# Small partition moves as maxima, weight halves by stage, and new prices in the ordering clock of a two-layer encoder

## The chip, the cores and the metric

The kernel runs on one core of a Trainium2 chip. The metric is the device time of one execution in microseconds (us), given as the median of several runs. A profiled execution of the same kernel gives the trace. The core's engines are named as in the profile: PE (matrix multiply, with PEld for its weight loads), DVE (VectorE), ACT (ScalarE), POOL (GpSimd) and SP (which issues the DMAs). Each engine works through its own instructions in order, and engines wait for each other by semaphores.

## The reference

Two layers of an encoder over 512 tokens of width 1024, in float32. Each layer, cut to what matters here:

```python
h = rms_norm(x, attn_norm_g)
c_q, c_kv, k_rope, gq, gk, gv, pool_in, gate_logits = split_columns(h @ w_in, IN_SIZES)
o_mla  = mla_branch(...)     # 8 heads, q and k of 96, v of 64, from latents of 256 and 128
o_gqa  = gqa_branch(...)     # 8 query heads, 2 key heads of 64
o_pool = pool_branch(...)    # centred means over 2, 4, 8, 16 tokens, minus the token
gates  = sigmoid(gate_logits)
merged = gates[0]*(o_mla @ w_b0) + gates[1]*(o_gqa @ w_b1) + gates[2]*(o_pool @ w_b2)
x = x + merged @ w_out
u_gate, u_val = split(depthwise_conv(rms_norm(x, ffn_norm_g) @ w_up))   # width 3, 2 x 2816 channels
x = x + (silu(u_gate) * u_val) @ w_down
```

Each attention computes `softmax(q k^T * scale) v` per head over all 512 keys.

## The kernel before

**Arithmetic.** Every float32 operand of a product is split into a high part, rounded by a copy to the format that PE reads in one pass, and a low part, the difference. A product is then three matmuls (`mm3`: high by high, high by low, low by high). Weights arrive from HBM in tiles `raw` and are split on the chip in `w_split`: `wh` by an ACT copy, `wl` by a subtraction on POOL or DVE. `pick` chooses the engine of `wl` from the modelled times at which the two come free, with `W_BIAS` in POOL's favour. `wnext` hands out one weight tile and keeps three more prepared ahead (`LA`).

**Stages of a layer.** In order: the latent projection, four pooling channels, the projections of the grouped-query attention (GQA), then the GQA heads, then the eight heads of the latent attention (MLA), then the output projection, then the feed-forward part. Beside the heads of both attentions runs a *filler*: units of three matmuls each that compute branch gates (`gate`) and branch projections (`branch`). A filler unit is put in wherever the heads have nothing ready. Some 48 further units follow the MLA heads.

**The order is made beforehand.** The instruction order of each engine is written out while the kernel is built. An ordering clock (`Clock`, and `Engine`, which wraps DVE, ACT and POOL) keeps a modelled time for PE and for each engine. `took` adds an instruction's modelled cost to its engine, `done` notes when a result will be there, and `chain` queues the steps of a chain of small instructions behind each other. `copy` puts a copy on ACT or DVE, whichever would end first by the model, with `C_BIAS` in ACT's favour. None of this is an instruction; it only decides which instruction comes after which, and on which engine. A matmul is priced at its columns divided by 2370, in us, and not below 0.107.

**An MLA head** is issued by `held_banks`, a list of tasks with conditions. Each round issues the first task that may go by the model; if none may, one filler unit is put in; if the filler has none left, modelled time passes with nothing issued. For head `h`:

- `a_part(h, k)`, four of them (line 1307): the high-by-high score product of one block of 128 keys into a PSUM bank, which stays held. Afterwards DVE takes maxima of it (`largest`, a transposing reduction, tile `nmt`).
- Behind the fourth: `over_keys` (maximum over the blocks, line 250), `gather` (three copies of 32 partitions by 16 values from the other three partition groups to the group in which the row is wanted, line 258), `over_groups` (a further maximum, tile `mrow`) and `row` (a DVE product that spreads the negated maxima into `qb`, line 242).
- `b_part(h, k)` (line 1348): two further products per bank; they need `qb` because the maximum is subtracted inside the product. They may be issued 0.4 us of modelled time after `qb` is due.
- `weights`: exponential on ACT, high copy `ph`, low part `pl`, and `vt` on DVE, which then releases the bank.
- `av_hi`, `av_lo`, `av_rest`: products with the values, 0.4 to 1.2 us after their operands are due.

`a_part` of the next head follows `b_part` of this one, and may not go before a quota of filler units is used. The quota is spread over the heads so that `late` units, the second number of `LEAD`, are left when the last head begins. Other work of a head on POOL: `qb` (low part of the queries), `kl` (low part of the keys) and `oraw` (a sum in the head's output). Lines 235, 242, 246, 250, 258, 266 are the helpers that record every ACT, DVE and POOL instruction; line 389 records nearly all matmuls.

Of the kernel before, what the change touches and what calls it, by code (L numbers as in the profile page):

```python
# [14 lines left out]
ALU = mybir.AluOpType  # L15
AX = mybir.AxisListType
PSUM = bass.MemoryType.PSUM

P = 128
T = 512  # L20
D = 1024
KC = D // P
# [22 lines left out]
RSQRT_BITS = 1597463007.0  # L45
SLACK = 35
PLAN = {"gqa": (-4.2, -1.0, -0.2, 0.0, 0.65, 2.411, 4.57, 32.003)}
LEAD = {"mla": (1.2, 22)}

D_OUT, D_IN, D_LAT = 3.2, 4.0, 6.0  # L50
D_FREE, D_SUM = 0.8, 2.0
REST = 0.4
W_BIAS = 2.54
C_BIAS = 0.2

PRM_AG, PRM_FG, PRM_PS, PRM_CQ, PRM_CKV = 0, 8, 16, 20, 22
PRM_W0 = 23
# [53 lines left out]
class Filler:  # L111


    def __init__(self, gen, total):
        self.gen, self.total, self.done = gen, total, 0
# [18 lines left out]
class Clock:  # L134
# [5 lines left out]
    def __init__(self):  # L140
        self.now, self.n, self.heap, self.busy = 0.0, 0, [], False
        self.fin, self.free, self.ready = 0.0, {}, {}
        self.source = self.last = None
        self.gives_way = {}

    def low(self, fn, most=4.0, engine="DVE"):
        self.gives_way[fn] = (engine, most)
        return fn
# [2 lines left out]
        heapq.heappush(self.heap, (self.now + dt, self.n, fn))  # L151
        self.n += 1

    def took(self, engine, cost):
        start = self.now + (0.0 if self.source is None else 0.13 if self.source == engine else self.SEM)
        self.free[engine] = max(start, self.free.get(engine, 0.0)) + cost
        self.last = engine
        self.fin = max(self.fin, self.free[engine])

# [17 lines left out]
    def done(self, *key):  # L177
        self.ready[key] = self.fin + self.SEM
# [36 lines left out]
class Engine:  # L215
# [4 lines left out]
    def __init__(self, ck, eng, kind):  # L220
        self.ck, self.eng, self.kind, self.table = ck, eng, kind, 0

    def _count(self, ap, per, fixed):
        n = 1
        for d in ap.shape[1:]:
            n *= d
        self.ck.took(self.kind, fixed + per * n)

    def activation(self, out, in_, func, **k):
        t = self.TABLE.get(func)  # L230
        if t and t != self.table and not (t == 2 and func is AF.Tanh and self.table == 3):
            self.table = t
            self.ck.took(self.kind, 1.28)
        self._count(out, 0.00084, 0.09 + 0.09 * (len(k) > 0))
        return self.eng.activation(out, in_, func, **k)  # L235

    def _two(self, out, *a):
        self._count(out, *((0.14, 0.1) if ALU.pow in a else (0.002145, 0.127) if self.kind == "Pool" else (0.00105, 0.07)))

    def tensor_tensor(self, out, *a):  # L240
        self._two(out, *a)
        return self.eng.tensor_tensor(out, *a)  # L242

    def scalar_tensor_tensor(self, out, *a):
        self._two(out)
        return self.eng.scalar_tensor_tensor(out, *a)  # L246

    def tensor_reduce(self, out, in_, *a, **k):
        self._two(in_)
        return self.eng.tensor_reduce(out, in_, *a, **k)  # L250

    def tensor_scalar(self, out, *a):
# [1 line left out]
        return self.eng.tensor_scalar(out, *a)  # L254

    def tensor_copy(self, out, in_, psum=False):
        self._count(out, 0.00105 if psum else 0.00053, 0.07)
        return self.eng.tensor_copy(out, in_)  # L258

    def reciprocal(self, out, in_):  # L260
# [13 lines left out]
def trunk(ctx: ExitStack, tc: tile.TileContext, x, w, prm, gb, cst, pad, out):  # L274
    nc = tc.nc
    ctx.enter_context(tc.manual_schedule())
    ck = Clock()
    at, need, done, chain, low = ck.at, ck.need, ck.done, ck.chain, ck.low
    V, A, G = Engine(ck, nc.vector, "DVE"), Engine(ck, nc.scalar, "ACT"), Engine(ck, nc.gpsimd, "Pool")
# [48 lines left out]
    def f(ap):  # L328
        return ap.bitcast(F32)
# [2 lines left out]
    pieces, swidth = _stream()  # L332
    soff = np.concatenate([[0], np.cumsum(swidth)]) * P
    st = {"dma": 0, "split": 0, "use": 0}
    raws, halves = {}, {}

    def w_dma():
        i = st["dma"]
        t = slot("raw") if i < KC else rawp.tile([P, 1024], F32, tag="raw", name=f"raw{i}")
        SY.dma_start(t[:, :swidth[i]], w[int(soff[i]):int(soff[i + 1])].rearrange("(p c) -> p c", p=P))  # L340
        raws[i] = t
        st["dma"] += 1

    def w_split():
        j = st["split"]
        sl, off, wd = pieces[j]
        while st["dma"] <= sl:
            w_dma()
        r = raws[sl][:, off:off + wd]
        hi = hlp.tile([P, T], F32R, tag="wh", name=f"wh{j}")  # L350
        lo = hlp.tile([P, T], F32R, tag="wl", name=f"wl{j}")
        ck.fin = ck.now
        if j == 0:
            V.tensor_copy(hi[:, :wd], r)
        else:
            A.activation(hi[:, :wd], r, AF.Copy)
        e = V if j < KC else G if j < KC + 3 else pick(W_BIAS, ck.fin + ck.SEM)
        ck.free[e.kind] = max(ck.free.get(e.kind, 0.0), ck.fin + ck.SEM)
        e.tensor_tensor(lo[:, :wd], r, f(hi[:, :wd]), ALU.subtract)
        done("w", j)  # L360
        if j + 1 == len(pieces) or pieces[j + 1][0] > sl:

            at(max(0.0, ck.free[e.kind] - ck.now) + D_FREE, lambda: w_upto(sl + 1 + RAW))
        halves[j] = (hi, lo)
        st["split"] += 1

    def pick(bias, t=0.0):

        t = max(t, ck.now)
        dve, pool = (max(t, ck.free.get(e, 0.0)) for e in ("DVE", "Pool"))  # L370
        return V if dve + 0.61 + bias < pool + 1.18 else G
# [15 lines left out]

    def mm(o, lhsT, rhs, start, stop):
        PE.matmul(o, lhsT=lhsT, rhs=rhs, start=start, stop=stop)  # L389
        ck.to(ck.now + max(0.107, rhs.shape[-1] / 2370.0))  # L390

    def turn(o, src):
        PE.transpose(o, src, ident)
        ck.to(ck.now + 0.107)

    def mm3(o, lh, ll, rh, rl, start, stop):
        mm(o, lh, rh, start, False)
# [118 lines left out]

    def copy(out, in_, psum=True, bias=C_BIAS):

# [40 lines left out]
    def layer(l, sq, xsrc):  # L559
# [194 lines left out]
        for b in range(4):  # L754
            v = slot("vg", F32R)
# [144 lines left out]
        now_mla = [False]  # L900
# [266 lines left out]
        def attention(kind, fill, okey, odst):  # L1167
# [135 lines left out]
            def a_part(h, k):  # L1303
                s = hs[h]
                tag, sc = sc_bank()
                s["sc", k] = (tag, sc)
                PE.matmul(sc, lhsT=s["ka"][:, k * P:k * P + P], rhs=s["qa"][:, :T], start=True, stop=True)
                ck.to(ck.now + T / 2370.0)
                if k == 0:
                    both = small("nmt", [P, P], bufs=1)  # L1310
                    s["pm"], s["pk"] = (both[:, c:c + 64].rearrange("p (k j) -> p k j", j=16) for c in (0, 64))
                base = 64 if gqa else 96

                def largest():
                    V.tensor_reduce(s["pm"][:, k], sc.rearrange("p (j r) -> p j r", r=32), AX.X, ALU.max,
                                    apply_transpose=True)

                def over_keys():
                    s["row"] = small("mrow", [P, 16], bufs=1)
                    V.tensor_reduce(s["pk"][:, 3], s["pm"].rearrange("p k j -> p j k"), AX.X, ALU.max)  # L1320

                def gather():
                    for g in range(4):
                        if 32 * g != base:
                            V.tensor_copy(s["pk"][base:base + 32, g if g < 3 else base // 32], s["pk"][32 * g:32 * g + 32, 3])

                def over_groups():
                    V.tensor_reduce(s["row"][base:base + 32], s["pk"][base:base + 32].rearrange("p g j -> p j g"), AX.X, ALU.max,
                                    negate=True)

                def row():
                    V.tensor_tensor(s["qb"][base:base + 32, :T].rearrange("p (j r) -> p j r", r=32),
                                    bc(s["row"][base:base + 32].unsqueeze(2), [32, 16, 32]),
                                    bc(ident[base:base + 32, None, base:base + 32], [32, 16, 32]), ALU.mult)
                    done(*key("m", h))

                chain(largest, *[over_keys, gather, over_groups, ([key("q", h)], row)] * (k == 3), after=0.3)

            def b_part(h, k):
                s = hs[h]  # L1340
                need(key("m", h), key("q", h))
                if not gqa:
                    need(key("kl", h))
                tag, sc = s.pop(("sc", k))
                kb_ = slice(k * P, k * P + P)
                pairs = [("kb", "qb")] if gqa else [("kb", "qa"), ("ka", "qb")]
                for n, (a_, b_) in enumerate(pairs):
                    PE.matmul(sc, lhsT=s[a_][:, kb_], rhs=s[b_][:, :T], start=False, stop=n == len(pairs) - 1,  # L1348
                              skip_group_check=True)
                    ck.to(ck.now + T / 2370.0)  # L1350
                weights(h, k, sc, lambda: sc_free(tag))

            def probs(h, k):
# [73 lines left out]
            def o_out(h):  # L1427
# [25 lines left out]

                steps = [low(copies, 1.5, "ACT") if kind in LEAD else copies]
                if h % 2 == 1:
# [15 lines left out]
            def held_banks():  # L1471
# [4 lines left out]

                lead, late = LEAD[kind]
                step = (fill.total - fill.done - late) / 7.0
# [133 lines left out]
        fb.upto(PRE_B)  # L1612
        while not ck.has(("tq", l, 0)) and fb.step():
            pass
        now_mla[0] = True
        attention("mla", fb, "om", omla)
        rest[0].finish()


        sq = slot("sq")  # L1620
# [56 lines left out]
        n = 0  # L1677
# [250 lines left out]
```

## Time and profile before

| what | value |
|---|---|
| median of 3 runs | 1572.32 us (1570.05 to 1575.77) |
| profiled execution | 1572.05 us |
| its span, first to last instruction | 1570.3 us, mean granted PE clock 0.999 |
| busy, share of the span: PE, DVE, ACT, POOL | 99%, 64%, 50%, 66% |
| HBM read and written | 151.50 MB and 13.63 MB, 105 GB/s |

A profile page gives the busy time of each engine, the groups of instructions by source line, and the waits. Its times are of one execution. A row of a group reads: line, engine, operation, output tile<-input tiles, shapes, count, then busy time and the mean of one in ns, then how long the engine stood idle before them and for whom. A row of a wait reads: engine, its tile and line, whom it waited for, then us in total, how often, and the longest. Durations of neighbouring instructions on one engine can overlap by a few hundredths of a us, and a matmul is drawn longer than its distance to the next.

### The profile page before, as it was taken

How to read it: one execution, taken by the hardware profiler on the slowest of the kernel's cores; microseconds unless marked ns; L12 is line 12 of the kernel's file. 1: busy time of each engine (PE TensorE's matmuls, PEld its weight loads, DVE VectorE, ACT ScalarE, POOL GpSimd, SP SyncE). 2: the span in 40 equal slices, each digit the busy share in tenths (PEclk: the TensorE clock that was granted, in tenths of full speed). 3: DMA queues.
4: the chain of work that ended last, by engine and by line, in shares of the span. 5: the costliest groups of instructions: out<-in, count | busy, mean ns of one | idle time of the engine just before them, and what ended most of it. 6: DMA issues, size and time to landing. Idle time of an engine off the chain costs nothing. (4 is left out here: it accounts for less than half of the span.)

```text
span 1570.3 us, 20451 instructions
## 1 busy us (share of the span) xinstructions
PE 1548.3 (99%) x7034; PEld 1288.0 (82%) x7034; DVE 1008.8 (64%) x1471; ACT 788.6 (50%) x1460; POOL 1032.4 (66%) x918
## 2 busy tenths in 40 slices
PE   9999999899999999999999999999999999999999
PEld 8878787778888888888898888877788888888888
DVE  6778889996267777711046788899862777776000
ACT  6557866664444444432244687756533444444221
POOL 4866986655667666654578669767546766666542
PEclk9999999999999999999999999999999999999999
DMA  5432234324323223333335222433252232332331
GB/s 201 126 113 74 75 111 141 101 91 136 106 94 100 100 97 94 94 120 109 114 106 135 93 79 70 147 116 112 69 157 98 86 102 94 96 100 99 108 129 46
DMA packets 82855, 166.46 MB, mean 106 GB/s; under 512 B 20928, under 2 KB 42944, under 8 KB 82752
## 3 DMA queue, kind: packets, MB, share of 16 engines
q1 hardware_dynamic: 82464, 165.03, 34.1%
q8 instruction: 55, 0.90, 0.2%
q14 instruction: 48, 0.39, 0.1%
q10 hardware_dynamic: 288, 0.14, 0.0%
HBM read 151.50 MB, written 13.63 MB: 105 GB/s over the span
## 5 line engine op out<-in xcount | busy, mean ns | idle before, releaser
L242 POOL TENSOR_TENSOR wl<-raw,wh 128x512 fp32r<-128x512 f32 (+2 forms) x499 | 671.0, 1356 | 356.5 <-ACT wh L235 331.6
L235 ACT ACTIVATE wh<-raw 128x512 fp32r<-128x512 f32 (+2 forms) x521 | 309.1, 607 | 122.7 <-PE ps_ST L389 41.3
L246 DVE SCALAR_TENSOR_TENSOR a<-u,prm,a 128x511 f32<-128x511 f32 x176 | 246.4, 1401 | 93.0 <-ACT a L235 86.1
L389 PE MATMUL ps_acc<-HH,wl 128*128 128x512 f32 x592 | 230.9, 390 | 0.4 <-POOL wl L242 0.4
L389 PE MATMUL ps_acc<-HH,wh 128*128 128x512 f32 x592 | 231.3, 391 | 0.0
L389 PE MATMUL ps_acc<-HL,wh 128*128 128x512 f32 x592 | 230.9, 390 | 0.0
L389 PEld LDWEIGHTS ps_acc<-HH,wl 128*128 128x128 f32 x592 | 111.3, 188 | 24.3 <-POOL wl L242 0.9
L389 PEld LDWEIGHTS ps_acc<-HH,wh 128*128 128x128 f32 x592 | 111.5, 188 | 22.9 <-issue 0.3
L389 PEld LDWEIGHTS ps_acc<-HL,wh 128*128 128x128 f32 x592 | 111.4, 188 | 22.9
L242 POOL TENSOR_TENSOR al<-a,ah 128x512 fp32r<-128x512 f32 x44 | 57.8, 1314 | 84.9 <-ACT ah L235 84.9
L389 PE MATMUL ps_AV<-HH,wh 128*128 128x512 f32 x288 | 112.3, 390 | 0.0
L389 PE MATMUL ps_AV<-HH,wl 128*128 128x512 f32 x288 | 112.1, 389 | 0.0
L389 PE MATMUL ps_AV<-HL,wh 128*128 128x512 f32 x288 | 112.1, 389 | 0.0
L389 PE MATMUL ps_ST<-HH,wh 128*128 128x512 f32 x240 | 93.5, 390 | 0.0
L389 PE MATMUL ps_ST<-HL,wh 128*128 128x512 f32 x240 | 93.4, 389 | 0.0
L389 PE MATMUL ps_ST<-HH,wl 128*128 128x512 f32 x240 | 93.4, 389 | 0.0
L235 ACT ACTIVATE ah<-a 128x512 fp32r<-128x512 f32 x44 | 27.8, 632 | 127.1 <-DVE a L242 127.1
L235 ACT ACTIVATE a<-a 128x512 f32<-128x512 f32 x44 | 27.8, 633 | 110.0 <-DVE a L246 110.0
L235 ACT ACTIVATE a<-u,prm 128x512 f32<-128x512 f32 x88 | 70.9, 808 | 20.8 <-DVE u L242 20.6
L235 ACT ACTIVATE HH<-XM,prm 128x512 fp32r<-128x512 f32 x32 | 23.1, 722 | 101.6 <-DVE XM L242 53.9
L235 ACT ACTIVATE gt<-gt 128x512 f32<-128x512 f32 x48 | 30.2, 630 | 75.5 <-DVE gt L242 73.3
L389 PEld LDWEIGHTS ps_AV<-HH,wl 128*128 128x128 f32 x288 | 54.1, 188 | 11.3
(415 smaller groups left out, 3798.4 us busy)
## 6 DMA issues: line engine op xcount, KB each, us to landing
raw<-w SPq DMA_DIRECT2D x228, 512.0 KB, 3.5
raw<-w SPq DMA_DIRECT2D x13, 384.0 KB, 3.0
XM<-x SPq DMA_DIRECT2D x16, 256.0 KB, 3.4
dtq<-tr SPq DMA_DIRECT2D x16, 192.0 KB, 1.9
dtk<-tr SPq DMA_DIRECT2D x16, 192.0 KB, 2.3
tf<-dtq SPq DMA_DIRECT2D x48, 64.0 KB, 2.3
tf<-dtk SPq DMA_DIRECT2D x48, 64.0 KB, 2.1
raw<-w SPq DMA_DIRECT2D x6, 448.0 KB, 3.4
```

The source lines that it names most:

```text
L235: return self.eng.activation(out, in_, func, **k)
L242: return self.eng.tensor_tensor(out, *a)
L246: return self.eng.scalar_tensor_tensor(out, *a)
L389: PE.matmul(o, lhsT=lhsT, rhs=rhs, start=start, stop=stop)
```

## The change

Four things are changed.

- `gather` uses `tensor_reduce` with a maximum over an added axis of length one in place of `tensor_copy`. The values are the same.
- While the MLA heads run, `wl` always goes to POOL (`pool_only`), without asking `pick`.
- The ordering clock gets other prices: matmuls, ACT instructions, short reductions, SBUF copies. DVE instructions whose operands all lie in SBUF, and POOL instructions, are now modelled as shutting each other out (`lock`): one that starts while the other kind runs ends that much later.
- Two numbers: `C_BIAS` 0.2 becomes 0, and the filler units left for the last MLA head 22 become 14.

```diff
-LEAD = {"mla": (1.2, 22)}
+LEAD = {"mla": (1.2, 14)}
-C_BIAS = 0.2
+C_BIAS = 0.0
...
-    def took(self, engine, cost):
+    def took(self, engine, cost, lock=None):
         start = self.now + (0.0 if self.source is None else 0.13 if self.source == engine else self.SEM)
-        self.free[engine] = max(start, self.free.get(engine, 0.0)) + cost
+        start = max(start, self.free.get(engine, 0.0))
+        self.free[engine] = start + cost
+        if lock is not None:
+            begun, over = self.locked
+            if begun <= start < over:
+                self.free[engine] = max(self.free[engine], over + cost - lock)
+            self.locked = (start, self.free[engine])
...
-    def _count(self, ap, per, fixed):
+    def _count(self, ap, per, fixed, ins=None):
...
-        self.ck.took(self.kind, fixed + per * n)
+        lock = None
+        if ins is not None and self.kind != "ACT":
+            if self.kind == "Pool":
+                lock = 0.1
+            elif not any(a.space is PSUM for a in (ap, *ins)):
+                lock = 0.06
+        self.ck.took(self.kind, fixed + per * n, lock)
...
-        self._count(out, 0.00084, 0.09 + 0.09 * (len(k) > 0))
+        self._count(out, 0.00082, (0.08 if in_.space is PSUM else 0.107) + 0.1 * sum(not isinstance(v, float) for v in k.values()))
...
     def tensor_reduce(self, out, in_, *a, **k):
         self._two(in_)
+        if in_.shape[-1] <= 4:
+            self.ck.took(self.kind, 0.08)
         return self.eng.tensor_reduce(out, in_, *a, **k)
...
     def tensor_copy(self, out, in_, psum=False):
-        self._count(out, 0.00105 if psum else 0.00053, 0.07)
+        self._count(out, 0.00105, 0.07, ins=(in_,))
...
-        e = V if j < KC else G if j < KC + 3 else pick(W_BIAS, ck.fin + ck.SEM)
+        e = V if j < KC else G if j < KC + 3 or pool_only[0] else pick(W_BIAS, ck.fin + ck.SEM)
...
-        ck.to(ck.now + max(0.107, rhs.shape[-1] / 2370.0))
+        ck.to(ck.now + rhs.shape[-1] / 2400.0 + 0.0135)
...
-                ck.to(ck.now + T / 2370.0)
+                ck.to(ck.now + 0.2268)
...
                 def gather():
                     for g in range(4):
                         if 32 * g != base:
-                            V.tensor_copy(s["pk"][base:base + 32, g if g < 3 else base // 32], s["pk"][32 * g:32 * g + 32, 3])
+                            V.tensor_reduce(s["pk"][base:base + 32, g if g < 3 else base // 32],
+                                            s["pk"][32 * g:32 * g + 32, 3].unsqueeze(2), AX.X, ALU.max)
...
-        now_mla[0] = True
+        now_mla[0] = pool_only[0] = True
         attention("mla", fb, "om", omla)
         rest[0].finish()
+        pool_only[0] = False
```

More of the change, by code (lines that the diff above doesn't have):

```diff
@@ L144, in __init__ @@
         self.gives_way = {}
+        self.locked = (0.0, 0.0)
     def low(self, fn, most=4.0, engine="DVE"):
@@ L233, in activation, with _two @@
             self.ck.took(self.kind, 1.28)
-        self._count(out, 0.00084, 0.09 + 0.09 * (len(k) > 0))
+        self._count(out, 0.00082, (0.08 if in_.space is PSUM else 0.107) + 0.1 * sum(not isinstance(v, float) for v in k.values()))
         return self.eng.activation(out, in_, func, **k)
-    def _two(self, out, *a):
-        self._count(out, *((0.14, 0.1) if ALU.pow in a else (0.002145, 0.127) if self.kind == "Pool" else (0.00105, 0.07)))
+    def _two(self, out, *a, ins=None):
+        self._count(out, *((0.14, 0.1) if ALU.pow in a else (0.002145, 0.127) if self.kind == "Pool" else (0.00105, 0.07)),
+                    ins=ins)
     def tensor_tensor(self, out, *a):
-        self._two(out, *a)
+        self._two(out, *a, ins=a[:2])
         return self.eng.tensor_tensor(out, *a)
     def scalar_tensor_tensor(self, out, *a):
-        self._two(out)
+        self._two(out, ins=(a[0], a[2]))
         return self.eng.scalar_tensor_tensor(out, *a)
@@ L334, in trunk @@
     st = {"dma": 0, "split": 0, "use": 0}
-    raws, halves = {}, {}
+    raws, halves, pool_only = {}, {}, [False]
     def w_dma():
@@ L389, in mm @@
         PE.matmul(o, lhsT=lhsT, rhs=rhs, start=start, stop=stop)
-        ck.to(ck.now + max(0.107, rhs.shape[-1] / 2370.0))
+        ck.to(ck.now + rhs.shape[-1] / 2400.0 + 0.0135)
     def turn(o, src):
         PE.transpose(o, src, ident)
-        ck.to(ck.now + 0.107)
+        ck.to(ck.now + 0.108)
     def mm3(o, lh, ll, rh, rl, start, stop):
@@ L1349, in b_part @@
                               skip_group_check=True)
-                    ck.to(ck.now + T / 2370.0)
+                    ck.to(ck.now + 0.2268)
                 weights(h, k, sc, lambda: sc_free(tag))
```

## The prediction

> **What bounds the kernel now.** I read the page first, then a table of stretches, then the waits of TensorE.
>
> ```profile
> span 1570.3 us, 20451 instructions
> PE 1548.3 (99%) x7034; PEld 1288.0 (82%) x7034; DVE 1008.8 (64%) x1471; ACT 788.6 (50%) x1460; POOL 1032.4 (66%) x918
> ```
>
> TensorE (PE) is busy for nearly all of the span, so a gain can only come out of the places where it stands still. The table of stretches finds them; its columns are length, then busy time (and instructions) of PE, PEld, VectorE (DVE), ScalarE (ACT) and GpSimd (POOL), clock, DMA share and GB/s.
>
> ```profile
> 60.00:108.00 48.00, 46.26 (x249) 39.71 (x248) 40.35 (x75) 28.14 (x62) 38.77 (x35) 1.00 0.41 114
> 108.00:200.00 92.00, 90.80 (x411) 74.49 (x410) 74.73 (x133) 70.81 (x137) 67.99 (x95) 1.00 0.26 80
> 228.00:346.00 118.00, 111.17 (x483) 88.92 (x482) 114.07 (x196) 71.71 (x135) 77.74 (x66) 1.00 0.38 117
> 385.00:780.00 395.00, 395.00 (x1745) 327.12 (x1744) 196.40 (x194) 160.93 (x269) 253.08 (x184) 1.00 0.33 103
> 840.00:890.00 50.00, 50.00 (x269) 43.84 (x269) 39.80 (x79) 28.95 (x63) 39.73 (x36) 1.00 0.38 114
> 890.00:975.00 85.00, 85.00 (x391) 71.23 (x390) 70.32 (x123) 70.23 (x135) 64.37 (x88) 1.00 0.24 74
> 1005.00:1123.00 118.00, 110.19 (x472) 88.50 (x472) 113.90 (x193) 69.92 (x132) 76.56 (x65) 0.99 0.39 117
> ```
>
> The third and last rows are the latent attention (MLA) of the two layers. There PE loses 6.8 and 7.8 us, and VectorE is busy 114 of 118 us. The feed-forward stretch (385 to 780) loses nothing. What PE waits for:
>
> ```profile
> PE ps_ST L1348 <- DVE qb L242: 6.8, 4, 1.9
> PE ps_AV L1348 <- DVE qb L242: 4.8, 4, 1.9
> PE ps_acc L389 <- DVE gt L246: 1.5, 2, 0.8
> PE ps_S L1348 <- DVE qb L242: 1.5, 2, 0.9
> ...
> PE ps_acc L389 <- POOL wl L242: 0.4, 1, 0.4
> ```
>
> Four rows, 12 waits, 14.6 us: ten are L1348 (`b_part`, the second product of a score bank) waiting for `qb`, the row of maxima that VectorE writes at the end of each head's chain. Before `qb` in that chain stand `gather`'s three copies. The chain of work that ended last, in one head (start, us, what; its last row here is from the feed-forward stretch and is used below), and GpSimd's timeline beside it:
>
> ```profile
> 1102.17 0.98 DVE nmt L258
> 1103.16 1.24 DVE nmt L258
> 1104.41 1.23 DVE nmt L258
> ...
> 1106.03 0.70 DVE qb L242
> ...
> 1174.16 5.44 PE ps_AV L389 x24
> ```
>
> ```profile
> 1101.83 1.29 POOL L242 TENSOR_TENSOR wl<-raw,wh 128x512 fp32r<-128x512 f32 x1 [1.82 <-ACT wh L235]
> 1103.08 1.29 POOL L242 TENSOR_TENSOR kl<-tf,kh 128x512 fp32r<-128x512 f32 x1
> 1104.33 1.28 POOL L242 TENSOR_TENSOR qb<-tf,qa 128x512 fp32r<-128x512 f32 x1
> ```
>
> Each L258 copy ends 0.03 us after a GpSimd instruction ends (1103.12, 1104.37, 1105.61): it waits for GpSimd, then does almost nothing. The tile's view gives the spread (ns, min/median/max):
>
> ```profile
> L258 DVE COPY nmt<-nmt x48: 167/982/1316, 234.4 to 1120.1; 32x16 f32<-32x16 f32 x48
> L250 DVE TENSOR_REDUCE nmt<-nmt x16: 217/268/274, 234.1 to 1118.4; 128x16 f32<-128x64 f32 x16
> L250 DVE TENSOR_REDUCE mrow<-nmt x16: 254/260/265, 235.5 to 1120.3; 32x16 f32<-32x64 f32 x16
> L242 DVE TENSOR_TENSOR qb<-mrow,C x16: 687/689/1436, 235.9 to 1120.6; 32x512 fp32r<-32x512 f32 x16
> ```
>
> A copy alone takes 167 ns and usually takes six times that. The 32 small maxima over the same tiles in the same chain never exceed 274 ns.
>
> **What the waits cost.** The wait view counts from the end of a matmul drawn 0.39 us long, but 24 matmuls take 5.44 us (the chain's last row), 0.227 us each. PE's timeline and the windows around one wait show the rest of the price:
>
> ```profile
> 1104.48 0.39 PE L1348 MATMUL ps_AV<-qa,kl 128*128 128x512 f32 x1
> 1106.77 0.50 PE L1348 MATMUL ps_AV<-qb,kh 128*128 128x512 f32 x1 [1.90 <-DVE qb L242]
> ```
>
> ```profile
> 1104.40:1107.80 3.40, 1.50 (x7) 0.91 (x6) 3.22 (x5) 0.46 (x2) 1.20 (x1) 1.00 0.39 133
> 1107.80:1111.20 3.40, 3.40 (x9) 2.63 (x8) 3.05 (x7) 3.40 (x8) 2.34 (x4) 0.50 0.00 0
> ```
>
> So each wait hides 0.39 - 0.227 = 0.163 us more (12 x 0.163 = 2.0), and the matmul behind it runs 0.50 instead of 0.39 us (12 x 0.11 = 1.3). After this one, the longest, the granted clock is 0.50 for 3.4 us, half of it lost, 1.7 us. Together 14.6 + 2.0 + 1.3 + 1.7 = 19.6 us. This is nearly all that the change can win.
>
> A rule of the Trainium skill speaks to the last term: "TensorE: Matmul & The Clock Gate", section "Why this matters for your kernels", allows idle gaps up to about 3 us before the clock drops. Here a gap of 2.29 - 0.23 = 2.06 us, in a window with PE busy 1.50 of 3.40 us, was followed by the half clock; by the page the 1.7 us would have another cause and stay, and the time would be 1.7 us longer. I go by the rows.
>
> **Part 1: `gather` as maxima over an axis of one.** The same three instructions per head, 48 in all, become reductions. This form (32x16 from 32x16x1) is not in the trace. Its lower bound is the free copy, 0.167 us; its upper bound the largest small maximum, 0.274 us, which reads four times as much. I take the middle, 0.22, so 0.66 us a head. The bounds could only be broken upward if these reductions waited for GpSimd too; that is a rival. The copies' group in one MLA stretch, with the other two groups that the change moves:
>
> ```profile
> L258 DVE COPY nmt<-nmt 32x16 f32<-32x16 f32 x24 | 18.1, 756 | 0.5
> ...
> L242 DVE TENSOR_TENSOR wl<-raw,wh 128x512 fp32r<-128x512 f32 x2 | 2.4, 1184 | 0.1
> ...
> L242 POOL TENSOR_TENSOR wl<-raw,wh 128x512 fp32r<-128x512 f32 x25 | 32.7, 1311 | 21.7 <-ACT wh L235 20.5 <-PE ps_AV L1307 0.8 <-POOL wl L242 0.3
> ```
>
> VectorE loses 18.1 - 24 x 0.22 = 12.8 us per layer. In the head above, 3.45 us of copies become 0.66: 2.8 us earlier against a stall of 2.06, so it vanishes. A head in which only one copy was held saves about 1.2 - 0.2 = 1.0 us, and the shortest stalls (0.75 us in the row of `ps_S`, and 0.163 hidden) are as long, so a little can be left; and `qb` itself still collides at times (1.436 against 0.689). I put back 0.5 us for that. What is late next is the ScalarE exponential and then PE's own order; no row shows either of them 2 us behind.
>
> The skill has a rule against this edit: "VectorE: DVE Perf Modes", "Rules for kernel authors", calls `tensor_reduce` on a hot path the slowest VectorE operation and advises another form. The trace agrees as to a free copy (0.217 to 0.274 against 0.167), not as to one beside a busy GpSimd. If the rule decided, 48 x 0.1 = 4.8 us would be added instead of the stalls removed, 1577 us.
>
> **Part 2: weight halves on GpSimd in the MLA stretch.** Before, VectorE took two `wl` in the second layer's stretch (the row above, 1.18 us each). GpSimd takes them at 1.31: 76.6 + 2.6 = 79 of about 108 us, 73%. Behind a `wl` on GpSimd's in-order queue stand `kl`, `qb` of the next head and `oraw`; PE needs them only a head later, and a `wl` is prepared three tiles ahead, 3 x 12 x 0.227 = 8.2 us. Cost on the path 0; uncovered, at most 4 x 1.31 = 5.2 us for both layers. VectorE ends at 113.9 - 12.8 - 2.4 = 98.7 of 108 us, no longer the engine that sets the pace.
>
> **Part 3: the ordering clock.** It adds no instruction; it changes the order. A matmul is now counted 0.2268 us (before 512/2370 = 0.216), which is what the 24-matmul row measures. The old clock ran PE 5% fast, so a real chain had 5% more time than planned: 0.0108 us a matmul, about 0.4 us over the 40 matmuls between a head's first score and its `qb`. That lead is lost. Against it, waits for GpSimd are now in the plan. `C_BIAS` 0 lets a copy go to VectorE 0.2 us sooner, with ScalarE at 70 of 118 us. Outside MLA I can only bound it: the same code in the two layers, ordered differently, loses 1.7 + 1.2 us (rows 60 to 200) and 0.0 (rows 840 to 975). So 2.9 us either way; I take 0, since the feed-forward rows show PE at 100% under very different loads of the others.
>
> **Part 4: `LEAD` 22 to 14.** Eight fewer filler units stay for the last head, each 3 matmuls. In the last head of the first layer, `ps_acc` alone from its first score product to its last value product:
>
> ```profile
> 330.70:351.70 21.00, 15.66 (x61) 11.50 (x62) 1.44 (x3) 0.00 (x0) 1.00 0.17 53
> ```
>
> 61 matmuls, 20 units, covered that head. With 14, 61 - 42 = 19 matmuls x 0.227 = 4.3 us of cover go, less 1.0 us by which the chain is shorter: at most 3.3 us of PE standing still per layer, at least 0 if the slower heads before it leave VectorE less behind. I take the middle, 1.65 per layer, 3.3 us.
>
> **The sum.** The profiled execution took 1572.05 us: 1572.05 - 19.6 + 0.5 + 3.3 = 1556.25. The median of the runs, 1572.32, is 0.27 above that execution, so 1556.5.
>
> **The rivals.** *The maxima wait as the copies do.* Then the stalls stay, and with part 4 the time is 1572.3 + 3.3 = 1575.6, no change. Against it: 32 small reductions in a stretch where GpSimd is busy 65% of the time, none over 274 ns. Chance 0.04. *Half of the stalls come back* elsewhere on VectorE, since it is still busy 91% of the stretch: 9.8 us back, about 1566.5. Chance 0.11. *Weight halves come late from GpSimd:* 5.2 us back, 1561.7; against it, PE waited for a `wl` 0.4 us in all. Chance 0.03. *Slower: the plan has lost its lead.* If `b_part` is now placed so early that `qb` misses it in all 16 heads, each pays for it. The point of no gain is (19.6 - 3.8)/16 = 1.0 us per head behind the plan, beyond its margin of 0.4. With today's worst wait everywhere, 2.06 + 0.11 = 2.2 us, it is 16 x 2.2 = 35 us: 1556.5 + 35 = 1591.5. For it: VectorE's queue is full and the 5% are gone. Against it: 12 waits in 16 heads leave four heads that met the plan even with the copies, and the plan now prices what was held. Chance 0.07.
>
> **How the numbers follow.** The forecast has the remaining 0.75. About 0.3% (4.7 us) is what a measurement can tell from no change. Own bounds of the forecast: all terms good, 1572.3 - 19.6 - 2.9 = 1549.8; all bad, 1572.3 - 19.6 + 0.5 + 6.6 + 2.9 + 5.2 = 1567.9. The range 1550 to 1568 takes in the second and third rivals too and leaves out the other two (0.11) and a tail on either side of the forecast (0.07). Faster: 0.75 + 0.11 + 0.03 less 0.02 for what ends above 1567.6, 0.87; same: 0.04 + 0.02 = 0.06; slower 0.07.
>
> **What would show it.** Right: the line that was L258 on `nmt` becomes a reduction of 0.17 to 0.27 us, 48 times, with no long ones; PE's waits for `qb` fall from 13.1 us to under 2; VectorE is busy at most 93% of the MLA stretches; no half clock at 1107; the first layer's last head shows PE idle up to 3 us before its last value products. Wrong: reductions of 1 us, new PE waits for `qb` or `wl` of over 5 us, or idle PE in the feed-forward rows.

## The result, and the profile after

The changed kernel takes 1561.17 us (median of 4 runs, 1560.56 to 1561.7), the kernel before 1573.78 us in the same measurement. The ratio is 0.9922, with a 95% interval of 0.9902 to 0.9943: about 12 us faster. The forecast was 1556.5 us, 1550 to 1568. The direction and the main step hold; two terms of the sum do not. They err in opposite directions, and that part of the error cancels is luck. The profiled execution takes 1560.56 us, its span is 11.5 us shorter. In the first group of runs below, one of the ten of the kernel before took 7014.56 us; without it the median there is 1571.88 instead of 1572.19 us, so that differences from it shift by 0.3 us.

The page, the stretches (columns as before; the first two rows are the GQA heads of the two layers, the next two their MLA heads, then the feed-forward part), and all of PE's waits:

```profile
span 1558.8 us, 20414 instructions
PE 1547.1 (99%) x7034; PEld 1286.1 (83%) x7034; DVE 991.3 (64%) x1470; ACT 790.6 (51%) x1459; POOL 1038.5 (67%) x920
```

```profile
105.00:232.00 127.00, 124.05 (x560) 100.44 (x559) 105.71 (x191) 94.40 (x185) 95.38 (x129) 1.00 0.27 85
881.00:1006.00 125.00, 122.82 (x557) 99.80 (x556) 104.30 (x188) 95.22 (x186) 95.36 (x129) 1.00 0.28 85
232.00:345.00 113.00, 112.51 (x492) 91.77 (x491) 105.35 (x196) 72.68 (x135) 81.04 (x68) 1.00 0.39 116
1006.00:1118.00 112.00, 111.77 (x492) 91.76 (x491) 104.26 (x195) 72.90 (x136) 80.85 (x68) 1.00 0.39 121
...
385.00:780.00 395.00, 395.00 (x1745) 327.12 (x1744) 194.72 (x189) 157.90 (x263) 251.66 (x182) 1.00 0.32 103
```

```profile
PE ps_S L405 <- POOL qa L256: 1.9, 2, 1.0
PE ps_ST L405 <- POOL qb L256: 1.4, 4, 0.4
PE ps_mi L1773 <- DVE warm L286: 1.1, 1, 1.1
PE ps_acc L405 <- DVE XM L260: 0.7, 2, 0.4
PE ps_acc L405 <- DVE MQ L274: 0.6, 1, 0.6
PE ps_acc L405 <- DVE gt L260: 0.6, 2, 0.3
PE ps_acc L405 <- ACT wh L248: 0.5, 1, 0.5
PE ps_acc L405 <- DVE gt L256: 0.4, 2, 0.2
PE ps_ST L1323 <- DVE vt L260: 0.3, 1, 0.3
```

No row names the maxima's `qb` from VectorE any more: 13.1 us of it are gone. The MLA stretches lose 0.5 and 0.2 us (before 6.8 and 7.8). But GQA loses 2.95 and 2.18 us, and in the kernel before it lost 1.20 and 0.04:

```profile
104.00:231.00 127.00, 125.80 (x578) 103.97 (x577) 105.68 (x194) 96.33 (x189) 97.60 (x134) 1.00 0.29 89
883.00:1008.00 125.00, 124.96 (x580) 104.64 (x579) 103.58 (x193) 99.30 (x192) 96.72 (x133) 1.00 0.29 88
```

The instructions themselves, in the groups by form and then in the timelines of VectorE and GpSimd around one head:

```profile
L266 DVE TENSOR_REDUCE nmt<-nmt 32x16 f32<-32x16 f32 x48 | 7.8, 162 | 1.0
L266 DVE TENSOR_REDUCE nmt<-nmt 128x16 f32<-128x64 f32 x16 | 4.3, 269 | 0.5
...
L256 DVE TENSOR_TENSOR qb<-mrow,C 32x512 fp32r<-32x512 f32 x16 | 17.3, 1078 | 0.9
```

```profile
1077.96 0.81 DVE L266 TENSOR_REDUCE nmt<-nmt 128x16 f32<-128x64 f32 x4
1078.81 0.26 DVE L266 TENSOR_REDUCE mrow<-nmt 32x16 f32<-32x64 f32 x1
1079.10 0.69 DVE L256 TENSOR_TENSOR gt<-ps_acc,rbc 128x512 f32<-128x512 f32 x1
1079.82 1.17 DVE L256 TENSOR_TENSOR qb<-mrow,C 32x512 fp32r<-32x512 f32 x1
```

```profile
1077.83 1.31 POOL L256 TENSOR_TENSOR kl<-tf,kh 128x512 fp32r<-128x512 f32 x1
1079.14 1.30 POOL L256 TENSOR_TENSOR wl<-raw,wh 128x512 fp32r<-128x512 f32 x1
```

The 48 small moves went from 36.1 us (17.9 and 18.1 in the two layers) to 7.8. Four reductions in a row take 0.81 us while GpSimd works on `kl` all the time. `qb` now meets GpSimd in its place: its mean went from 737 to 1078 ns, but no matmul waits for it.

**A count by stage.** To add stages up I count each matmul by the distance to the next start, less columns/2400 + 0.0135 us, the distance that undisturbed ones have. That includes what a wait hides, the slower matmul behind it, and half clock (stretches in which the granted clock is 0.50). The sum fell from 32.0 to 20.5 us, the 11.5 us by which the span is shorter. In us, first and second layer:

| kernel | before the heads | GQA | MLA | MLA to output projection | all |
|---|---|---|---|---|---|
| before | 6.0, 0.8 | 3.3, 0.9 | 9.6, 11.7 | 0, 0 | 32.0 |
| changed | 3.7, 0.7 | 6.6, 5.5 | 1.6, 0.7 | 0.8, 0.8 | 20.5 |
| maxima alone | 4.6, 0.8 | 3.2, 0.9 | 2.3, 2.2 | 0, 0 | 13.8 |
| copies back | 3.4, 0.7 | 6.6, 5.6 | 14.6, 10.7 | 0.8, 0.8 | 43.2 |
| old matmul price | 3.4, 0.7 | 11.5, 11.2 | 4.7, 4.8 | 2.5, 1.1 | 39.8 |
| wait not priced | 6.2, 0.6 | 6.0, 6.3 | 1.3, 1.9 | 0.2, 0.2 | 22.7 |
| new clock in MLA alone | 5.3, 0.9 | 3.2, 1.0 | 2.4, 0.2 | 0.8, 0.8 | 14.6 |
| + matmul price everywhere | 4.3, 0.7 | 4.7, 4.9 | 1.0, 2.2 | 0.8, 0.8 | 19.4 |
| + wait priced everywhere | 3.9, 0.7 | 13.5, 11.5 | 1.9, 3.2 | 0.9, 0.9 | 36.4 |

How much of such a count is chance can be seen where two kernels have the same order of instructions. Before the first layer's heads the kernel before and the kernel with the maxima alone have it, and count 6.0 and 4.6 us. The changed kernel and the kernel with `pick` in MLA (below) have it throughout, and count 20.5 and 21.7 us in all. A difference of 1 us between two rows says little. The step from 4.2 to 12.1 us in GQA is far beyond that.

### The profile page after: what moved, and what is told of

Its sections match the earlier page's. It is cut to its first block, busy times and chain, and to the rows that moved or that the text cites. A ratio compares the mean times of both kernels' runs of the same rounds, so it can differ in the third digit from the quotient of the medians.

```text
span 1558.8 us, 20414 instructions
## 1 busy us (share of the span) xinstructions
PE 1547.1 (99%) x7034; PEld 1286.1 (83%) x7034; DVE 991.3 (64%) x1470; ACT 790.6 (51%) x1459; POOL 1038.5 (67%) x920
## 4 chain that ended last, share of the span: by engine, by line
PE 89%; ACT 3%; DVE 3%; POOL 3%; issue 1%; DMA 0%; SPq 0%; POOLq 0%; ACTq 0%; DVEq 0%
PE ps_acc L405 39%; PE ps_AV L405 22%; PE ps_ST L405 20%; PE ps_S L405 2%; PE ps_mi L405 2%; PE ps_ST L1365 1%; POOL qa L256 1%; DVE XM L256 1%; ACT ps_ST L248 1%; DVE mgl L256 0%; POOL oraw L256 0%; ACT wh L248 0%; PE ps_ST L1323 0%; PE ps_mi L1365 0%; ACT qa L248 0%
## 5 line engine op out<-in xcount | busy, mean ns | idle before, releaser
L256 POOL TENSOR_TENSOR wl<-raw,wh 128x512 fp32r<-128x512 f32 (+3 forms) x501 | 672.3, 1353 | 382.9 <-ACT wh L248 342.0
L405 PEld LDWEIGHTS ps_AV<-HH,wh 128*128 128x128 f32 x288 | 54.1, 188 | 11.1
```

## The experiments

All times are medians of device time. In each group of runs the kernel before was measured too: 1572.19, 1572.58 and 1572.37 us in the three groups.

### The instruction or the order

**The maxima alone**, in the order of before. Apart from the 48 instructions the sequence of every engine is that of the kernel before.

```diff
-                            V.tensor_copy(s["pk"][base:base + 32, g if g < 3 else base // 32], s["pk"][32 * g:32 * g + 32, 3])
+                            o_ = s["pk"][base:base + 32, g if g < 3 else base // 32]
+                            V._count(o_, 0.00053, 0.07)
+                            V.eng.tensor_reduce(o_, s["pk"][32 * g:32 * g + 32, 3].unsqueeze(2), AX.X, ALU.max)
```

> The kernel before, with its instruction order kept to the last instruction; only the 48 copies of gather become maxima over an axis of one (priced in the clock as the copies were, so that nothing else moves). Theory 'instruction': the gain comes from these 48 alone and the new order costs about 5 us a layer in the GQA stretch, so this kernel is faster than the changed one: 1573 - 19.6 = 1552 to 1556 us, PE waits for qb under 2 us. Rival 'order': the gain comes from the new clock having priced the waits; then this stays within 5 us of the kernel before, 1568 to 1574 us.

Measured: 1554.6 us, ratio 0.9897 (0.9881 to 0.9914). The view of tile `nmt` (ns, min/median/max), and what is left of the waits in PE's wait view:

```profile
L1327 DVE TENSOR_REDUCE nmt<-nmt x48: 161/162/165, 233.0 to 1101.4; 32x16 f32<-32x16 f32 x48
```

```profile
PE ps_ST L1350 <- DVE qb L242: 1.0, 2, 0.5
...
PE ps_mi L1350 <- DVE qb L242: 0.2, 1, 0.2
```

The instruction alone wins 17.6 us, more than the whole change. It beats the changed kernel by 6.6 us.

**The copies back**, in the order of the changed kernel, again with every other instruction in its place.

```diff
-                            V.tensor_reduce(s["pk"][base:base + 32, g if g < 3 else base // 32],
-                                            s["pk"][32 * g:32 * g + 32, 3].unsqueeze(2), AX.X, ALU.max)
+                            i_ = s["pk"][32 * g:32 * g + 32, 3]
+                            V._two(i_)
+                            V.ck.took(V.kind, 0.08)
+                            V.eng.tensor_copy(s["pk"][base:base + 32, g if g < 3 else base // 32], i_)
```

> The changed kernel, with its instruction order kept; only the 48 maxima of gather become copies again (priced in the clock as the maxima). Theory 'instruction': the waits for qb come back, 13 to 20 us, 1574 to 1581 us, copies of about 0.7 us on average. Rival 'order': the new order leaves room for the copies, 1561 to 1565 us.

Measured: 1582.3 us, ratio 1.0072 (1.0057 to 1.0087). The same two views:

```profile
L1344 DVE COPY nmt<-nmt x48: 167/574/1284, 235.3 to 1129.9; 32x16 f32<-32x16 f32 x48
```

```profile
PE ps_acc L405 <- DVE gt L256: 8.1, 5, 2.6
PE ps_ST L1367 <- DVE qb L256: 7.9, 6, 2.0
```

21.1 us come back, against 17.6 in the other pair. The new order with the old instruction is slower than the kernel before. Of the 16.0 us in these two rows half fall on `gt`, a filler's eviction that here stands behind the copies on VectorE. Both pairs say the same: the 48 instructions are the gain, and the order made with the new prices gives some of it away.

### Which of the edits does what

**22 filler units for the last head** in the changed kernel.

```diff
-LEAD = {"mla": (1.2, 14)}
+LEAD = {"mla": (1.2, 22)}
```

> The changed kernel with 22 filler units instead of 14 left for the last MLA head. The prediction's fourth part: 14 leaves up to 3.3 us per layer of PE standing still in the last head, so 22 wins up to 6.6 us. The profile of the changed kernel shows no such idle time, which says 0: 1560 to 1562 us. Rival 'spacing': the 14 spaces the heads and so keeps the waits for qb away; then 22 brings back some of them, 1563 to 1570 us.

Measured: 1561.26 us, ratio 0.9938 (0.9924 to 0.9953). It makes no difference to the time, and neither the prediction's fourth part nor the rival is borne out. It does change how the last head runs; the section on the prediction uses that.

**Weight halves of the MLA stretch placed by `pick` again.**

```diff
-        e = V if j < KC else G if j < KC + 3 or pool_only[0] else pick(W_BIAS, ck.fin + ck.SEM)
+        e = V if j < KC else G if j < KC + 3 else pick(W_BIAS, ck.fin + ck.SEM)
```

> The changed kernel with the low weight halves of the MLA stretch placed by pick again. The prediction's second part costs this edit at nothing on the path: 1560 to 1563 us, a few wl on VectorE in the MLA stretch. Rival 'it keeps VectorE free': MLA waits of 1 to 3 us a layer come back, 1563 to 1568 us. Rival 'GpSimd is made late by it': faster by up to 5 us, 1556 to 1560 us.

Measured: 1561.24 us, ratio 0.9927 (0.9912 to 0.9942). The sequences of instructions of the two kernels are the same, line for line: with the new prices `pick` sends every one of these halves to GpSimd by itself, so none is on VectorE, where a few were expected. The edit is empty beside the others. Its 1561.24 against 1561.17 us is also a measure of how far two runs of one program differ.

**The old matmul price** in the changed kernel.

```diff
-        ck.to(ck.now + rhs.shape[-1] / 2400.0 + 0.0135)
+        ck.to(ck.now + max(0.107, rhs.shape[-1] / 2370.0))
...
-                ck.to(ck.now + 0.2268)
+                ck.to(ck.now + T / 2370.0)
...
```

> The changed kernel with the old prices for matmuls alone (columns/2370, not below 0.107, in the clock). Theory 'lost lead': the waits that the changed kernel shows in the GQA stretch (about 5 us in each layer) come from the clock no longer running PE 5% fast; then they shrink to 1 to 2 us a layer and the time is 1553 to 1557 us, with the MLA stretch still free of waits. Rival 'other prices': they come from the prices of ACT and of VectorE against GpSimd; then the time stays 1559 to 1563 us.

Measured: 1577.28 us, ratio 1.0036 (1.0019 to 1.0054). Both theories missed: GQA lost 11.5 and 11.2 us, twice as much as in the changed kernel. In the MLA stretch the last head ran out of cover; PE's timeline, with its last four value products:

```profile
348.61 1.52 PE L405 MATMUL ps_AV<-pl,vm 128*128 128x512 f32 x3
351.85 0.80 PE L405 MATMUL ps_AV<-vt,unit 128*128 128x512 f32 x1 [1.73 <-DVE vt L260]
```

Here the shortage that the prediction's fourth part describes does occur, with the last value product drawn 0.80 us long in half clock.

**The wait of VectorE and GpSimd not priced** in the changed kernel.

```diff
-        self.ck.took(self.kind, fixed + per * n, lock)
+        self.ck.took(self.kind, fixed + per * n)
```

> The changed kernel with its clock not pricing the wait of VectorE and GpSimd for each other (all other new prices kept). The instructions are the same. Open is which of the new prices makes the waits of about 5 us a layer in the GQA stretch. Theory 'it is the wait's price': they vanish and the MLA stretch stays as good as the fast maxima make it, 1552 to 1556 us. Rival 'it is another price': GQA loses 5 us a layer as now, 1559 to 1563 us; and should the price be what keeps the MLA stretch free of waits, that stretch gets 2 to 6 us a layer worse, 1565 to 1573 us.

Measured: 1562.05 us, ratio 0.9929 (0.9911 to 0.9946). GQA 6.0 and 6.3, MLA 1.3 and 1.9 us: this price is neither the cause of the loss nor what keeps MLA free of waits.

**`C_BIAS` back at 0.2** in the changed kernel (`-C_BIAS = 0.0`, `+C_BIAS = 0.2`).

> The changed kernel with C_BIAS back at 0.2: a copy goes to ScalarE unless VectorE would end more than 0.2 us sooner. In the changed kernel VectorE makes 12 of the copies ph of the second layer's GQA stretch, in the kernel with the maxima alone 7. Theory 'copies on VectorE hold up GQA': GQA loses 1 to 3 us a layer instead of 5.5 to 6.6, 1553 to 1557 us. Rival: within 2 us of the changed kernel, 1559 to 1563 us.

Measured: 1561.31 us, ratio 0.9928 (0.9911 to 0.9946). GQA lost 5.7 and 6.0 us; not the cause.

### The new prices in one stage, and one at a time

**The new clock in the MLA stretch alone.** A flag `ck.mla` is set where `pool_only` is set; each price, `C_BIAS` among them, is the new one where it is set and the old one elsewhere.

```diff
-        ck.to(ck.now + rhs.shape[-1] / 2400.0 + 0.0135)
+        ck.to(ck.now + (rhs.shape[-1] / 2400.0 + 0.0135 if ck.mla else max(0.107, rhs.shape[-1] / 2370.0)))
...
-        self.ck.took(self.kind, fixed + per * n, lock)
+        self.ck.took(self.kind, fixed + per * n, lock if self.ck.mla else None)
...
-        now_mla[0] = pool_only[0] = True
+        now_mla[0] = pool_only[0] = ck.mla = True
...
```

> The changed kernel with its new prices, C_BIAS 0 among them, in force only while the MLA heads are ordered; the rest of the layer is ordered with the old prices, as in the kernel before. Theory 'the new prices help in MLA and hurt in GQA': GQA as before (3.2 and 0.9 us lost), MLA as in the changed kernel (1.6 and 0.7 us lost), so a little faster than the kernel with the maxima alone (1554.6): 1551 to 1554 us. Rival 'they help nowhere': 1554 to 1558 us.

Measured: 1554.18 us, ratio 0.9883 (0.9867 to 0.9898). Up to the first layer's MLA heads the order of instructions is that of the kernel before, and with the old prices GQA loses 3.2 and 1.0 us, as there: so the new prices do cost GQA its order. In MLA the count is 1.9 us below that of the maxima alone (4.5 to 2.6), and 1.6 above it behind the heads. The total cannot be told from the kernel with the maxima alone, and by the time the rival is not out.

From this kernel, one new price at a time was put in force everywhere, each by dropping its `if ck.mla`.

**The matmul price.** 

> The kernel with the new clock in the MLA stretch alone, and of the new prices one, that of matmuls, in force everywhere. Theory 'lost lead': with PE priced at its true length GQA loses 4 to 7 us a layer, as in the changed kernel, 1560 to 1565 us. Rival 'the prices have to fit each other, no single one is to blame': GQA stays at 1 to 3.5 us a layer, 1553 to 1557 us.

Measured: 1560.32 us, ratio 0.9926 (0.9898 to 0.9955). GQA loses 4.7 and 4.9 us, 5.4 more than without.

```profile
PE ps_ST L409 <- POOL qb L260: 1.0, 1, 1.0
PE ps_S L409 <- DVE nm L270: 1.0, 1, 1.0
PE ps_S L409 <- POOL qa L260: 0.9, 1, 0.9
```

These are the second layer's GQA waits: short ones, each for an operand that came about 1 us later than PE was ready to use it. Whether the clock had held these operands to be ready is not shown.

**The wait of VectorE and GpSimd.** 

> The same kernel with only the wait of VectorE and GpSimd for each other priced everywhere. Taking this price out of the changed kernel left its GQA stretch as it was, so theory 'not this price': GQA 1 to 3.5 us a layer, 1553 to 1557 us. Rival 'any change of the prices costs GQA its order': 4 us a layer or more, 1560 us or more.

Measured: 1575.79 us, ratio 1.002 (1.0009 to 1.0032). The rival's figure: GQA loses 13.5 and 11.5 us. Longer waits this time, second layer:

```profile
PE ps_acc L409 <- DVE vm L260: 2.0, 1, 2.0
PE ps_ST L409 <- POOL MK L260: 1.9, 1, 1.9
```

**`C_BIAS` 0.** 

> The same kernel with only C_BIAS 0 everywhere. Putting it back in the changed kernel left GQA as it was, so theory 'not this one': 1553 to 1557 us. Rival 'any change costs GQA its order': 4 us a layer or more, 1560 us or more.

Measured: 1553.63 us, ratio 0.9884 (0.9855 to 0.9913). GQA loses 2.3 and 2.4 us: not this price.

**The ScalarE prices.** 

> The same kernel with only the new ScalarE prices everywhere. They differ from the old by some hundredths of a us an instruction. Theory 'lost lead': 1553 to 1557 us. Rival 'any change costs GQA its order': 4 us a layer or more, 1560 us or more.

Measured: 1555.05 us, ratio 0.9893 (0.9864 to 0.9922). GQA loses 4.7 and 2.2 us, the first of them as much as the rival said, but MLA only 0.3 and 0.7, so the sum stays. `C_BIAS` and these prices leave the time where it was. The new prices of short reductions and of SBUF copies were not tried alone.

**What follows.** The true matmul price costs GQA 5 us in both layers together when it is the only one, and up to 8 with the rest. The price of the wait costs nothing beside the true matmul price (12.1 us in GQA with it, 12.3 without), but about 20 beside the old one: 22.7 and 25.0 us in the two kernels that combine them. In the second of these, 5.1 of the 25.0 us are half clock (three stretches of 3.4 us in the GQA heads). So these two prices have to fit each other, and the waits of GQA are not the fault of one. Shown is which of the prices tried move the loss. That the lost 5% of lead makes the short waits fits the run with the matmul price alone and is not shown beyond it. The code fits it too: the products of an MLA head go 0.1 to 1.2 us of modelled time after their operands are due, while the GQA heads go by fixed positions (`PLAN`, the same in both kernels) with no such margin. No run here changes `PLAN` or gives GQA a margin, so the cause stays open, and so does why the wait's price does so much harm beside the old matmul price.

## Why the prediction was right or wrong

**The main step was right.** The 12 waits, priced at 19.6 us with what they hide, were the cost of the copies' waits for GpSimd. MLA gave 19.0 us back in the changed kernel (21.3 to 2.3 in the table) and 16.8 in the kernel with the maxima alone. The first rival, that the maxima wait as the copies do, is out: 48 of them, 161 to 165 ns in the kernel with the maxima alone.

**Part 1** took 0.22 us, the middle of its bounds; measured 0.162, just below the lower bound of 0.167. The rule weighed there, that a reduction is the slowest VectorE operation (the Trainium skill, "VectorE: DVE Perf Modes", "Rules for kernel authors"), does not show at this size: 162 ns against 167 for a copy alone. The 0.5 us put back for collisions of `qb` was not needed in the changed kernel: `qb` collides more often, mean 1078 ns, and no wait is left; in the kernel with the maxima alone 1.2 us of them stayed. VectorE was put at 91% of the MLA stretches; it is at 93% (105.35 of 113 us), and still does not set the pace.

**Part 2** cost the weight halves at nothing on the path. That came out, but it was hardly put to the test: beside the other edits this one changes no instruction.

**Part 3 is where the sum failed.** It took 0 with 2.9 us either way for the order outside MLA. Measured were 7.9 us more in GQA (4.2 to 12.1), 1.6 behind MLA, 2.4 less before the heads: 7.1 us more, over twice its bound. (Of the 2.4 us, 1.3 also appear between two kernels with the same order there, so that part may be chance.) The bound came from two layers ordered with one set of prices; that says how much chance differs, not what a systematic shift does, and the changed kernel loses in both layers (6.6 and 5.5 us). The step had named the lost 5% of lead, but put it only against `qb` in MLA, where the margin is 0.4 us. The feed-forward rows, 395.00 of 395.00 us before and after, were right but said nothing about GQA.

**Part 4** put 3.3 us on the last head's cover; measured 0. Rows of the changed kernel, the window of the first layer's last head with `ps_acc` alone, and the matmuls at its beginning; then the same window in the kernel with 22 units:

```profile
330.20:344.80 14.60, 10.75 (x45) 8.08 (x44) 0.73 (x2) 0.00 (x0) 1.00 0.15 45
```

```profile
323.48 0.39 PE L1365 MATMUL ps_S<-qb,kh 128*128 128x512 f32 x1
330.28 0.62 PE L1323 MATMUL ps_ST<-qa,kh 128*128 128x512 f32 x2
330.74 0.39 PE L1323 MATMUL ps_mi<-qa,kh 128*128 128x512 f32 x1
330.96 0.39 PE L1323 MATMUL ps_S<-qa,kh 128*128 128x512 f32 x1
```

```profile
323.20:344.40 21.20, 15.38 (x61) 11.55 (x62) 1.37 (x2) 0.00 (x0) 1.00 0.16 50
```

The cover fell nearly as worked out, from 61 matmuls to 45 (worked out: 42). The step failed in taking the head's length as unchanged but for 1.0 us. The quota now holds the last head's first score product back until 6.8 us after the previous head's last one (323.48 to 330.28). Its four score products then come within 0.7 us, and the head needs 14.6 us instead of 21. That this is the quota's doing is shown by the kernel with 22 units, in which only this number was set back: there the first score product follows 0.2 us behind the previous head, the four are spread over 6.4 us, and the head takes 21.2 us with 61 matmuls of cover. The shortage is real only where fewer units are left and the head is still long, as in the kernel with the old matmul price (21.2 us, 14 units).

**Half clock.** The 1.7 us went away with the wait. That a gap of about 2 us can go with it, against the 3 us of the rule in the Trainium skill ("TensorE: Matmul & The Clock Gate", "Why this matters for your kernels"), is seen again in three of the kernels above. In the kernel with the copies back no product starts between 1064.72 and 1067.29; the window with this gap and the one behind it:

```profile
1064.60:1068.00 3.40, 1.22 (x6) 0.70 (x5) 3.28 (x6) 0.73 (x2) 1.70 (x2) 1.00 0.00 0
1068.00:1071.40 3.40, 3.40 (x10) 2.64 (x9) 2.13 (x5) 1.56 (x4) 2.90 (x3) 0.50 0.48 158
```

**The sum.** Forecast -19.6 + 0.5 + 3.3 = -15.8 us; measured in the profiles -11.5, made of -19.0 in MLA and +7.1 elsewhere, the rest being rounding and feed-forward. The missing 4 us are the new waits of GQA in part 3, partly made up by the last head's cover that was not needed. That the two errors offset each other was luck. Two small slips in the working: the second rival's terms, 1556.5 + 9.8, make 1566.3 us, not 1566.5, and the shortest of the two stalls given as 0.75 us is 0.61 us, 0.75 being their mean; neither changes a step.

## What to carry to other kernels

An instruction that does almost nothing can hold up a chain for a GpSimd instruction's whole length; compare its longest time with its shortest, and look for a form of it that keeps its shortest time beside a busy GpSimd. When a change alters both an instruction and the rule that orders the instructions, run each with the other held fixed: here the instruction alone won 17.6 us and the order gave 6.6 of it back. A truer price in an ordering model is not by itself a better order: here the true matmul price alone cost GQA about 5 us. A likely reason, not shown here, is that the plans and margins beside it were chosen with the old errors in them.

## What the runs showed of the hardware that was not expected

The small maxima are not only free of the wait, they are at 161 to 165 ns no slower than a copy alone (167 ns). Ten times, in the profiles of before and of three experiments, half clock came with a standstill of PE of 2.0 to 2.8 us; it lasted 3.4 us, twice 6.8 us, and in four of the ten it began before the standstill ended. Six other standstills of 2.0 to 2.7 us had none, among them 2.2 us (at 1084, copies back) and 2.7 us (at 1001, old matmul price). What decides between the two is not shown.
